# Gate products moved behind the state chains of a running head, in a two-layer decoder trunk on one core

## The chip, the cores and the metric

One core of a Trainium2 chip runs the whole program. Its engines work side by side and wait for one another by semaphores: TensorE (PE in the profile, its weight loads PEld), VectorE (DVE), ScalarE (ACT), GpSimd (POOL), and SyncE (SP), which here only issues transfers. The metric is the device time of one execution in microseconds (us), the median of several runs.

## The reference

Two layers act on 1024 tokens of width 1024, in float32. The first mixes the tokens with a gated linear recurrence of 8 heads, the second with a causal convolution module; a squared-ReLU MLP follows each, with post-normalisation. The change lies in the first mixer alone:

```python
def hgrn2_mixer(h, w_in, lb, norm_g, w_out):
    proj = h @ w_in
    q, fz, v, g = jnp.split(proj, 4, axis=-1)
    q = jax.nn.silu(q)
    f = lb + (1.0 - lb) * jax.nn.sigmoid(fz)
    log_f = jnp.log(jnp.maximum(f, GATE_EPS))
    k = 1.0 - f
    ...
    bc = jnp.cumsum(to_chunks(log_f, dk), axis=-2)
    o = chunkwise_gated_recurrence(qc, kc, vc, bc)   # S = diag(f) S + k v^T, o = S^T q
    o = o * lax.rsqrt(jnp.mean(jnp.square(o), axis=-1, keepdims=True) + RMS_EPS)
    o = o * norm_g.reshape(H, dv)
    o = o.reshape(B_, S_, D) * jax.nn.silu(g)
    return o @ w_out
```

The product in the last line but one, `o * silu(g)`, is what the change moves.

## The kernel before

**Order.** In this stage the program writes out the order of every engine by hand. TensorE runs 12 pairs of weight blocks (8 pairs of q and forget gate, `"q"`, one for each head; 4 pairs of output gates, `"g"`, each for two heads). Each pair is seven products, the forms 1, 2, 6, 5, 7, 3, 4 of a Strassen-like scheme (`ORDER`), and each product is 12 matmuls over four weight tiles. After each weight tile `slot()` runs: one tick of a counter `ticks[0]`. Work of other engines is put off by ticks with `later(n, job)`, and every call is recorded in the order in which it is made, so a job that is put off later stands later in its engine's queue.

**Forms and buffers.** `make_form` builds the weight forms: ScalarE casts a block `pr` into `fs` (L634), VectorE subtracts the cast to get the low part. `evacuate` takes the products out of PSUM. For the forms 1, 6 and 5 ScalarE copies the bank into one of four buffers `t` (L857); later forms are added to it by VectorE. Forms 1, 6, 7 and 4 accumulate in one and the same bank, so form 7 can start only when the copy of form 6 has read it. The four buffers `t` (t_755 to t_758 in the rows below) rotate: after a pair of output gates they hold the four gates `silu(g)` (two heads, two halves of the tokens), and the next pair writes them again.

**Recurrence.** Between the matmuls of the pairs, `step()` advances up to two heads at once, each by one stage of the generator `recurrence(h)`; `one[2]` in `active` counts the stages of a head. In stage 13 TensorE transposes the keys, and in stage 14 it makes the outer products of keys and values, from which VectorE forms a chain of four states (`state`: a copy and three multiply-adds). One stage later the state matmuls of TensorE use them (`ps<-state,qk`), and a second chain of three follows. Then ScalarE sums the squares of the head's outputs (L755), GpSimd raises them to the power -1/2 (L756, L538), ScalarE scales the outputs (L761), TensorE turns them (`ps<-ident,o`), ScalarE scales them again (L774), and SP writes them to memory (`od`).

**Gates.** `gate_turn()` runs on each tick. It reads an output back from `od` into one of two buffers `u`, and when the gate is there and nine ticks have passed since the read was issued, VectorE multiplies (`t<-u,t`); two ticks later SP stores the product (`zd<-t`):

```python
        if loaded and loaded[0][0] in gates and loaded[0][2] <= now - 9:
            (h, half), u, _ = loaded.pop(0)
            g = gates.pop((h, half))
            mul(g, u, g)
```

This happens 12 times, for six heads; the last two heads take another way. SP issues all transfers of this stage in one order: blocks `pr`, values `v`, outputs `od`, returned outputs `u`, products `zd`.

**Weight sums.** GpSimd's queue also carries transfers that sum blocks of the MLP's second weights in memory (`sum_w`, L419 to L423), one after another, each waiting for an earlier one to land. They stand in the same queue as GpSimd's part of the recurrence.

Of the kernel before, what the change touches and what calls it, by code (L numbers as in the profile page):

```python
# [268 lines left out]
def body(ctx, tc, d, out):  # L269
# [114 lines left out]
    def later(n, job):  # L384
        if n:
            waiting.append((ticks[0] + n, job))
        else:
            job()
# [252 lines left out]
    qk, gates, vts = {}, {}, {}  # L641

    def mul(o, a, b):
        vector.tensor_tensor(out=o, in0=a, in1=b, op=ALU.mult)
# [182 lines left out]
    recs, active, pace, alone = [], [], [0.0, 0.0], [False]  # L827
# [94 lines left out]
    def slot():  # L922
        tick()
        gate_turn()
        pace[0] += pace[1]
        if pace[0] >= 1:
            pace[0] = pace[0] - 1 if step() else 0.0

    to_load, loaded, to_gate = [], [], []

    def gate_turn():
        now = ticks[0]
        if to_load and len(loaded) < 2 and done.get(to_load[0], now) <= now - 7:
            at = to_load.pop(0)
            u = p1("u")
            nc.sync.dma_start(out=u, in_=od[at[0]][at[1]])
            loaded.append((at, u, now))
        if loaded and loaded[0][0] in gates and loaded[0][2] <= now - 9:
            (h, half), u, _ = loaded.pop(0)
            g = gates.pop((h, half))  # L940
            mul(g, u, g)

            def store():
                nc.sync.dma_start(out=zd[half][:, h, :], in_=g)
                stored[h, half] = ticks[0]

            later(2, store)
# [1035 lines left out]
```

## Time and profile before

| | |
|---|---|
| median of 3 runs | 2057.65 us (2055.35 to 2061.02) |
| profiled execution | 2057.38 us, its span 2055.6 us |
| PE busy | 2024.2 us (98%) |
| DVE busy | 1488.7 us (72%) |
| ACT busy | 1092.3 us (53%) |
| POOL busy | 394.7 us (19%) |
| the recurrence's stage, 98 to 425 us | PE busy 317.71 of 327.00 us |
| the twelve products `t<-u,t` | DVE, median 691 ns, from 198.2 to 392.9 us |

The span runs from the first to the last instruction; the time of the execution has a little on either side of it. A row of the timeline gives the start, the duration, the engine, the source line, the operation with its output and inputs, how many like it were merged, and in brackets how long the engine had stood idle before it and what ended that. Operations that go through the clock-keeping wrapper all carry the line L204, so they are told apart by their tiles. A row of waits gives the waiting instruction, what it waited for, the total in us, how often, and the longest.

### The profile page before, as it was taken

Reading aid. Unit: us, or ns where it says so; the run is one execution under the profiler, and the core shown is the slowest. Engines: PE = TensorE matmul, PEld = TensorE weight load, DVE = VectorE, ACT = ScalarE, POOL = GpSimd, SP = SyncE. Lnnn points to the kernel's source line nnn. Section 1 sums busy time; section 2 is a strip of 40 time slices with the busy share of each in tenths; the row PEclk is TensorE's granted clock in tenths of the full one; section 3 lists DMA queues with packets and bytes.
Section 4 is the critical chain, followed back from the end, with each engine's and each line's share of the span. In section 5 each row is a group of like instructions: output and inputs, shape, how many; then the busy total and the mean of one; then the engine's idle time right before and its main releaser. Section 6 shows DMA issues by size and latency. Waiting matters only on the chain. (4 is left out here: it accounts for less than half of the span.)

```text
span 2055.6 us, 29682 instructions
## 1 busy us (share of the span) xinstructions
PE 2024.2 (98%) x11144; PEld 1669.3 (81%) x11144; DVE 1488.7 (72%) x1978; ACT 1092.3 (53%) x1725; POOL 394.7 (19%) x405
## 2 busy tenths in 40 slices
PE   8999999999999999999999999999999999999998
PEld 7888887888788888888888888888888888888886
DVE  8698887877866665666557898889589666754456
ACT  5456565631654655444443776488615555443343
POOL 0112232111000000000001799079210000100002
PEclk9999999999999999999999999999999999999999
DMA  4788999942399786999998755487659778995542
GB/s 187 216 206 229 263 244 250 268 185 89 125 324 298 275 302 215 374 341 325 336 339 294 303 185 187 191 329 268 255 210 344 247 236 299 392 293 195 194 154 103
DMA packets 183120, 517.55 MB, mean 252 GB/s; under 512 B 17984, under 2 KB 49856, under 8 KB 181824
## 3 DMA queue, kind: packets, MB, share of 16 engines
q1 hardware_dynamic: 167488, 456.93, 61.7%
q0 software_dynamic: 15488, 58.72, 12.3%
q8 instruction: 87, 1.43, 0.3%
q14 instruction: 57, 0.47, 0.1%
HBM read 380.85 MB, written 201.85 MB: 283 GB/s over the span
## 5 line engine op out<-in xcount | busy, mean ns | idle before, releaser
L204 PE MATMUL ps<-dw,dh 128*128 128x512 f32 x2688 | 611.6, 389 | 0.9 <-ACT dh L72 0.7
L204 PEld LDWEIGHTS ps<-dw,dh 128*128 128x128 f32 x2688 | 504.1, 188 | 106.3 <-ACT dh L72 1.1
L204 PE MATMUL ps<-x1f,fw 128*128 128x512 f32 x1344 | 307.8, 390 | 4.3 <-ACT fw L72 2.9
L204 PEld LDWEIGHTS ps<-x1f,fw 128*128 128x128 f32 x1344 | 251.4, 188 | 59.2 <-issue 2.7
L204 PE MATMUL ps<-xf,fs 128*128 128x512 f32 x1008 | 250.0, 399 | 3.5 <-issue 1.9
L204 POOL TENSOR_TENSOR cb<-cb,prod 128x512 f32<-128x512 f32 x168 | 222.5, 1333 | 14.4 <-ACT prod L1614 4.1
L204 PEld LDWEIGHTS ps<-xf,fs 128*128 128x128 f32 x1008 | 184.8, 189 | 42.8 <-issue 2.1
L204 DVE TENSOR_TENSOR dh<-dh 128x1024 fp32r<-128x1024 f32 x112 | 136.3, 1222 | 109.6 <-ACT dh L72 106.5
L204 DVE SCALAR_TENSOR_TENSOR ps<-u,par,ps 128x512 f32<-128x512 f32 x296 | 205.9, 749 | 10.7 <-ACT ps L1626 9.3
L204 PE MATMUL ps<-xa,wa 128*128 128x512 f32 x864 | 203.6, 393 | 1.3 <-DVE xa L204 0.9
L72 ACT CAST dh<-dh 128x1024 fp32r<-128x1024 f32 x112 | 117.2, 1050 | 146.3 <-DMA dh<-hf 141.2
L204 DVE TENSOR_TENSOR dw<-dr,dw 128x1024 fp32r<-128x1024 f32 x112 | 136.2, 1222 | 76.2 <-ACT dw L72 75.5
L204 PEld LDWEIGHTS ps<-xa,wa 128*128 128x128 f32 x864 | 160.2, 188 | 35.1 <-DVE xa L204 1.3
L72 ACT CAST dw<-dr 128x1024 fp32r<-128x1024 f32 x112 | 117.1, 1052 | 134.7 <-PE ps L204 114.0
L1614 ACT ACTIVATE prod<-u,par 128x512 f32<-128x512 f32 x168 | 119.2, 725 | 35.4 <-POOL cb L204 34.8
L538 POOL TENSOR_TENSOR mv<-mv,nhalf 128x1 f32<-128x1 f32 x32 | 42.2, 1319 | 403.9 <-DVE mv L204 393.6
L204 PE MATMUL ps<-w,oT 128*128 128x512 f32 x384 | 89.9, 392 | 1.3 <-ACT oT L952 0.8
L204 PE MATMUL ps<-xb,wa 128*128 128x512 f32 x384 | 91.1, 393 | 0.0
L204 PE MATMUL ps<-vw,xf 128*128 128x512 f32 x336 | 79.4, 398 | 6.1 <-ACT vw L455 5.5
L204 PEld LDWEIGHTS ps<-w,oT 128*128 128x128 f32 x384 | 71.4, 188 | 16.6 <-ACT oT L952 1.2
L204 PEld LDWEIGHTS ps<-xb,wa 128*128 128x128 f32 x384 | 71.1, 188 | 14.4
L1465 ACT CAST spare<-next 128x1024 fp32r<-128x1024 f32 x38 | 39.9, 1051 | 78.0 <-DMA next<-in_wpw_dram 23.9
(252 smaller groups left out, 2915.3 us busy)
## 6 DMA issues: line engine op xcount, KB each, us to landing
wa<-ready SPq DMA_DIRECT2D x140, 512.0 KB, 4.4
dh<-hf SPq DMA_DIRECT2D x112, 512.0 KB, 4.7
sum_w<-in_w_dram POOLq DMA_DIRECT2D x40, 1024.0 KB, 10.8
ready<-spare SPq DMA_DIRECT2D x76, 512.0 KB, 5.0
raw<-in_w1q_dram SPq DMA_DIRECT2D x66, 512.0 KB, 4.6
dr<-sum_w SPq DMA_DIRECT2D x64, 512.0 KB, 7.4
hf<-ht SPq DMA_DIRECT2D x112, 256.0 KB, 6.1
dr<-in_w_dram SPq DMA_DIRECT2D x48, 512.0 KB, 6.9
```

The source lines that it names most:

```text
L72: self.nc.scalar.copy(out=slot[:, 0, c], in_=raw[:, c])
L204: return op(*args, **kw)
L538: nc.gpsimd.tensor_tensor(out=dst, in0=src, in1=nhalf[:, :n], op=ALU.pow)
L1465: nc.scalar.copy(out=slot[:, 0].bitcast(F32R), in_=raw)
L1614: nc.scalar.activation(tp, u[:, k : k + HT], AF.Copy, scale=tap(j, k))
```

## The change

While any running head has reached stage 13 or 14, a product is held until 18 ticks after its output's read was issued; otherwise until nine, as before.

```diff
@@ -935,7 +935,8 @@
             u = p1("u")
             nc.sync.dma_start(out=u, in_=od[at[0]][at[1]])
             loaded.append((at, u, now))
-        if loaded and loaded[0][0] in gates and loaded[0][2] <= now - 9:
+        busy = any(13 <= one[2] <= 14 for one in active)
+        if loaded and loaded[0][0] in gates and loaded[0][2] <= now - (18 if busy else 9):
             (h, half), u, _ = loaded.pop(0)
             g = gates.pop((h, half))
             mul(g, u, g)
```

On TensorE, ScalarE and GpSimd no instruction changes its place. On VectorE five of the twelve products move, in three places; on SP the stores of the products, and a few transfers beside them.

Place 1, VectorE, after the gates of heads 0 and 1 (rows of the difference; t_756 to t_758 are gate buffers, T_763 holds decay products of the younger head, fs and pr are a weight form and its block): ahead of the older head's first state stood two products.

```order
 L204 TENSOR_TENSOR fs_595<-pr_600,fs_595 128x512
-L204 TENSOR_TENSOR t_757<-u_762,t_757 128x512
 L204 SCALAR_TENSOR_TENSOR t_758<-ps_70,sq_760 128x512
-L204 TENSOR_TENSOR t_756<-u_761,t_756 128x512
 L204 COPY state_772<-ps_70 128x128
 L204 SCALAR_TENSOR_TENSOR state_773<-state_772,dec_775,ps_70 128x128
```

They now stand behind the second chain of that head, on both sides of an addition into t_755:

```order
 L204 TENSOR_TENSOR T_763<-T_763 128x64
+L204 TENSOR_TENSOR t_757<-u_762,t_757 128x512
 L204 TENSOR_TENSOR t_755<-t_755,ps_70 128x512
+L204 TENSOR_TENSOR t_756<-u_761,t_756 128x512
 L204 TENSOR_TENSOR fs_590<-pr_599,fs_590 128x512
```

Place 1, SP's queue (the line of the store differs by the line that the change adds): the store of t_756 stood among the first of these, and now stands behind the load of pr_599, which waits until VectorE has read that block's last use.

```order
 L605 DMA pr_600<-in_wp_dram 128x512
+L605 DMA pr_598<-in_wp_dram 128x512
 L936 DMA u_762<-od10_573 128x512
-L944 DMA zd1_588<-t_757 128x512
-L944 DMA zd1_588<-t_756 128x512
-L605 DMA pr_598<-in_wp_dram 128x512
+L945 DMA zd1_588<-t_757 128x512
 L605 DMA pr_599<-in_wp_dram 128x512
+L945 DMA zd1_588<-t_756 128x512
 L652 DMA v_779<-vd00_86 128x4x128
```

Both stores moved down past the load of pr_598, and that of t_756 past the load of pr_599 as well. ScalarE's next copy into t_756 is that of form 6 of the pair that runs then.

Place 2, VectorE, after the gates of heads 2 and 3: one product ahead of a first state.

```order
 L204 TENSOR_TENSOR fs_594<-pr_600,fs_594 128x512
-L204 TENSOR_TENSOR t_755<-u_762,t_755 128x512
 L204 COPY state_769<-ps_70 128x128
 L204 SCALAR_TENSOR_TENSOR state_770<-state_769,dec_776,ps_70 128x128
```

It moved behind that head's second chain. In place 3, after the gates of heads 4 and 5, one product moves from ahead of the first chain to between the first and the second.

## The prediction

> **What bounds the kernel now.** I read the page first, then two windows of the span, then what TensorE waits for inside the stage that the change touches.
>
> ```profile
> span 2055.6 us, 29682 instructions
> PE 2024.2 (98%) x11144; PEld 1669.3 (81%) x11144; DVE 1488.7 (72%) x1978; ACT 1092.3 (53%) x1725; POOL 394.7 (19%) x405
> ...
> 98.00:425.00 327.00, 317.71 (x3501) 262.56 (x3500) 272.38 (x442) 202.10 (x478) 73.80 (x86) 0.99 0.90 250
> ...
> PE ps L204 <- ACT o L761: 2.4, 3, 1.1
> PE ps L204 <- issue: 1.9, 1, 1.9
> PE ps L204 <- DVE state L204: 1.4, 2, 0.9
> ```
>
> TensorE is busy for 98% of the span, so time is won or lost only where it stands still. The row by windows is the stage of the pair products and the recurrence, 98 to 425 us: 327.00 - 317.71 = 9.3 us of TensorE idle, with the DMA engines at 0.90. That is 0.45% of the span, and no reordering here can win more. The last three rows are TensorE's longest waits from 140 to 432 us (total, times, longest). The wait that this change can remove is the third: twice, 1.4 us together, TensorE waits for the state chains. A result within 0.3% (6.2 us, about what a measurement of this kernel can tell from no change) is still "the same".
>
> **The change, place by place.** Nothing is added or removed; TensorE, ScalarE and GpSimd keep their orders. Of the 12 products of a gate with a returned output, five change position on VectorE, and their stores with them on SP's queue. There are three places.
>
> Place 1, near 218 us. Timeline rows (start, duration, and in brackets the idle time before):
>
> ```profile
> 217.08 0.68 DVE L204 TENSOR_TENSOR t<-u,t 128x512 f32<-128x512 f32 x1
> 217.68 0.68 DVE L204 SCALAR_TENSOR_TENSOR t<-ps,sq 128x512 f32<-128x512 f32 x1
> 218.28 0.68 DVE L204 TENSOR_TENSOR t<-u,t 128x512 f32<-128x512 f32 x1
> 218.88 0.28 DVE L204 COPY state<-ps 128x128 f32<-128x128 f32 x1
> ...
> 225.41 0.68 DVE L204 TENSOR_TENSOR fs<-pr,fs 128x512 fp32r<-128x512 f32 x1
> ...
> 217.68 0.60 PE L204 MATMUL ps<-v,at 128*128 128x128 f32 x4
> 219.22 0.49 PE L204 MATMUL ps<-state,qk 128*128 128x128 f32 x2 [0.94 <-DVE state L204]
> ```
>
> Two products stand right ahead of the first state; consecutive starts are 0.60 apart, so without them the copy of the state starts 1.20 us earlier, at 217.68, and ends near 217.96. TensorE is through with its four matmuls at 218.28. The 0.94 us wait goes whole. On VectorE the products return after the second chain, where the row at 225.41 again stands behind the same work and keeps its time.
>
> What is late next is what hangs on the products. The second one (buffer t_756) was done at 218.96 and is now done near 225.4. Its store stood among the first here, and in the new order it stands behind a load that waits for the row at 225.41:
>
> ```profile
> 218.16 1.15 SPq L944 DMA_DIRECT2D zd<-t  x2
> 223.34 3.12 SPq L605 DMA_DIRECT2D pr<-in_wp_dram  x2
> ...
> 228.12 0.64 ACT L857 COPY t<-ps 128x512 f32<-128x512 f32 x1
> ...
> 230.25 3.02 PE L204 MATMUL ps<-xf,fs 128*128 128x512 f32 x12
> ...
> pr<-in_wp_dram SPq DMA_DIRECT2D x2, 256.0 KB, 5.0
> ...
> u<-od SPq DMA_DIRECT2D x14, 256.0 KB, 3.6
> v<-vd SPq DMA_DIRECT2D x14, 256.0 KB, 9.9
> ...
> out_dram<-y SPq DMA_DIRECT2D x4, 256.0 KB, 2.0
> ```
>
> The second load of the pair ended at 223.34 + 3.12 = 226.46, so the store is issued at about 226.5 instead of before 219.31. ScalarE's copy at 228.12 writes the next form's sum into that same t_756 and must wait until the store has read it. Behind the copy on ScalarE stand a weight cast and the scaling of the head's outputs. The copy also empties the PSUM bank into which the product at 230.25 (form 7) accumulates. So the chain is store, copy, TensorE, and its length is the store's landing time, which the trace does not give for these stores. Four rows bound it for 256 KB: 2.0 (stores at the end of the kernel) and 9.9 (loads of the values), with 3.6 and 5.0 between. I take 5.0, because these are two transfers of the same size on the same queue in just this stretch (223 to 227 us). The store then lands at 231.5, the copy ends at 231.5 + 0.64 = 232.1, and form 7 starts 1.9 us later than before, although TensorE could have come at 230.25 - 0.94 = 229.31. At 2.0 the copy ends by 229.1 and 0.94 is kept; at 9.9 it ends at 237.0 and place 1 costs 6.8.
>
> The Trainium skill ("DMA: Bandwidth & Descriptors", section "Anatomy of one DMA") gives a fit, made on the gpsimd path, of about 2.0 us fixed plus bytes over 436 GB/s. By it 256 KB land in an estimated 2.6 us, the copy ends at 229.7 and place 1 wins 0.5 instead of losing 1.9; the loads at 5.0 in this stretch contradict it, and the final sum below comes out the same by both.
>
> VectorE's third product (t_758) moves a little too:
>
> ```profile
> 228.07 0.68 DVE L204 TENSOR_TENSOR t<-u,t 128x512 f32<-128x512 f32 x1
> ...
> 233.03 0.69 DVE L204 TENSOR_TENSOR fs<-pr,fs 128x512 fp32r<-128x512 f32 x1 [2.59 <-ACT fs L634]
> ...
> 360.86 0.59 ACT L857 COPY t<-ps 128x512 f32<-128x512 f32 x1
> ```
>
> It goes from 228.07 behind the subtraction at 233.03. ScalarE's delay reaches that subtraction as well, which then runs up to 2 us late, as TensorE does; VectorE sat idle 2.59 us ahead of it, so this adds nothing of its own. The reload of the u buffer waits for the first product and moves with it by some 6 us; what reads it is this third product, later still, so I cost it at nothing.
>
> Does the shift reach the end? The next wait of TensorE:
>
> ```profile
> 268.52 0.66 PE L204 MATMUL ps<-ident,o 128*128 128x128 f32 x4 [1.06 <-ACT o L761]
> ...
> 264.11 1.22 POOL L421 DMA_DIRECT2D sum_w<-in_w_dram  x1 [4.32 <-issue]
> 265.40 0.70 POOL L756 TENSOR_SCALAR ss<-ss 128x4 f32<-128x4 f32 x1
> 266.19 1.10 POOL L538 TENSOR_TENSOR ss<-ss,nhalf 128x4 f32<-128x4 f32 x1
> ...
> 267.32 1.14 ACT L761 ACTIVATE o<-ps,ss 128x128 f32<-128x128 f32 x4 [2.29 <-POOL ss L538]
> ```
>
> TensorE waits for ScalarE, ScalarE for GpSimd's power, and GpSimd's two operations start only when the DMA issue at 264.11 is through. That issue follows the landing of an earlier block copy: the weight sums on GpSimd's queue are a chain of transfers that does not ask where TensorE stands. So this point is a clock of its own. A lead of 0.94 is lost here (the wait becomes 2.0), and a lag of 1.9 shrinks by 1.06 to 0.8.
>
> Place 2, near 335 us, and the clock of GpSimd after it:
>
> ```profile
> 334.53 0.68 DVE L204 TENSOR_TENSOR t<-u,t 128x512 f32<-128x512 f32 x1
> 335.13 0.28 DVE L204 COPY state<-ps 128x128 f32<-128x128 f32 x1
> ...
> 335.47 0.49 PE L204 MATMUL ps<-state,qk 128*128 128x128 f32 x2 [0.51 <-DVE state L204]
> ...
> 380.62 0.86 POOL L423 DMA_DIRECT2D sum_w<-sum_w  x1 [10.90 <-DMA sum_w<-in_w_dram]
> 381.55 0.74 POOL L756 TENSOR_SCALAR ss<-ss 128x4 f32<-128x4 f32 x1
> ...
> 385.09 0.66 PE L204 MATMUL ps<-ident,o 128*128 128x128 f32 x4 [0.94 <-ACT o L761]
> ```
>
> One product ahead of the state goes behind the second chain: 0.60 earlier, more than the 0.51 that TensorE waited, so 0.5 us is won. Its store is then issued near 341.7, and its buffer is written again only by the copy at 360.86 (row above), 19 us later, so nothing waits for that one. At 385.09 the pattern of 268.52 returns: ScalarE's factor comes from GpSimd, which had waited 10.90 us for a DMA. 0.94 is absorbed.
>
> Place 3, near 372 us:
>
> ```profile
> 371.21 0.69 DVE L204 TENSOR_TENSOR t<-u,t 128x512 f32<-128x512 f32 x1
> 372.42 0.28 DVE L204 COPY state<-ps 128x128 f32<-128x128 f32 x1
> ...
> 376.94 1.11 DVE L204 SCALAR_TENSOR_TENSOR state<-state,dec,ps 128x128 f32<-128x128 f32 x3 [0.88 <-PE ps L204]
> ```
>
> Here TensorE does not wait for the state at all, and the product moves into a hole of 0.88 us ahead of the second chain. I cost it at nothing; its cover is that hole, and without it the second chain would start 0.60 later.
>
> **Sum.** Place 1 puts TensorE 1.9 later; 1.06 of it goes at 268.52, 0.8 stay; place 2 takes 0.5, 0.3 stay; at 385.09 they go into the 0.94. At the end 0.0. With a landing of 2.0 a lead arrives at both clocks and is lost there: again 0.0. The profiled execution took 2057.38, 1.8 above its span and 0.3 under the median of the three runs (2057.65), so the forecast is 2057.4.
>
> **Rivals.** Faster: the leads stay. This needs GpSimd's chain of weight sums to come earlier itself, which could be, since the stores leave 218 to 225 us, where the chain's transfers also run. Then 0.94 + 0.51 = 1.45 are won. A second source is a stall that the change might shift away:
>
> ```profile
> 347.28 1.49 PE L204 MATMUL ps<-xf,fs 128*128 128x512 f32 x4 [1.89 <-issue]
> ...
> 348.00:351.50 3.50, 3.50 (x12) 2.77 (x12) 1.92 (x5) 3.09 (x9) 1.00 (x1) 0.55 1.05 233
> ```
>
> TensorE stands 1.89 us in the middle of one product, waiting for nothing that the profile shows, and then runs 3.5 us at a granted clock of 0.55, which loses 3.5 x 0.45 = 1.6. If this goes, 3.5 us are won: 2053.9. Against it: nothing in the change touches that product. I price the rival at 2055.0, between the two gains.
>
> Slower: the late store. It decides from the landing time on. Covered are 230.25 - 0.64 - 226.5 = 3.1 us until form 7 is later than before, and 1.06 + 0.51 + 0.94 = 2.5 more by the later slack, so the end moves from a landing of 5.6 us on. At 9.9 the end is 4.3 later, 2061.7. The wait may also cost the clock: at 5.0 TensorE would idle 232.1 - 229.3 = 2.8 us, longer than the 1.89 after which the clock fell above, and 1.6 would come on top, 1.9 + 1.6 - 2.5 = 1.0 at the end, 2058.4. For the rival as a whole I take 2060. Over 0.3% slower it is only from 5.6 + 6.2 = 11.8 us of landing.
>
> On that clock the Trainium skill ("TensorE: Matmul & The Clock Gate", section "Why this matters for your kernels") says that gaps over about 3 us between bursts bring it down. By that page a stall of 2.8 us would be free and the 1.0 would not come; the row at 348 us, after 1.89 us of idle, speaks for the charge, and I leave it in the rival.
>
> No effect: the rule acts on too little. Only two of the five moved products had a wait behind them; if place 1's wait is not VectorE's order but the recurrence's own length, the time is also 2057.4. The rows at 217.08 to 218.88, back to back, speak against it.
>
> **How the numbers follow.** Likeliest, shifts absorbed: 0.58, 2057.4, own range 2055.5 to 2059.5, since the three runs differ by that much. No effect: 0.04, the same number. Faster rival: 0.17, of which 0.03 beyond 0.3%. Slower rival: 0.21, of which 0.04 beyond 0.3%. The range of 8 in 10 takes the low end of the faster rival, 2053.9, and the landing of 9.9, 2061.7. Faster 0.03, the same 0.93, slower 0.04.
>
> **What would show it.** In the new profile the two waits of the state matmuls (0.94 and 0.51) should be gone. Form 7's matmuls near 230 us should show a new wait of up to 2.8 us on ScalarE's copy into t, and that copy should start at about 231. The transposes near 268 and 385 us should again wait on ScalarE's outputs, and start within 1 us of the old times. I am wrong if the state waits remain, if the copy into t starts near 228 although the store is late, if TensorE's order near 268 or 385 no longer waits, or if the time moves by more than 6 us, which would say that a chain that I hold for paced by DMA is paced by TensorE.

## The result and the profile after

The changed kernel takes 2063.32 us (median of 22 runs, 2055.49 to 2068.91), the kernel before 2057.77 on the same chip (22 runs, 2054.29 to 2063.74). The ratio is 1.0026, 95% interval 1.0016 to 1.0035: 5.5 us slower, outside the forecast range. The profiled execution took 2062.3, with a span of 2060.5 against 2055.6. One of the twelve runs of e3 below took 2897.82 us at a granted clock of 0.65; it is left out of that kernel's ratio, and the other eleven have a median of 2060.90.

The page of the changed kernel, then TensorE's longest waits from 140 to 440 us (total, times, longest):

```profile
span 2060.5 us, 29679 instructions
PE 2024.0 (98%) x11144; PEld 1670.4 (81%) x11144; DVE 1487.8 (72%) x1978; ACT 1092.9 (53%) x1725; POOL 393.0 (19%) x405
...
PE ps L204 <- ACT t L857: 10.2, 2, 9.3
PE ps L204 <- issue: 1.3, 1, 1.3
```

TensorE's work is the same (2024.0 us). The waits for VectorE's state are gone from the list, and one wait of 9.3 us for ScalarE's copy into t has come. The timeline around it, first SP's queue and GpSimd, then ScalarE and TensorE:

```profile
224.79 0.43 SPq L945 DMA_DIRECT2D zd<-t  x1
226.22 0.33 SPq L605 DMA_DIRECT2D pr<-in_wp_dram  x1
226.60 0.47 SPq L945 DMA_DIRECT2D zd<-t  x1
...
225.67 0.92 POOL L423 DMA_DIRECT2D sum_w<-sum_w  x1 [2.58 <-DMA sum_w<-in_w_dram]
226.28 1.07 POOL L419 DMA_DIRECT2D sum_w<-in_w_dram  x1
229.49 0.76 POOL L420 DMA_DIRECT2D sum_w<-in_w_dram  x1
...
238.08 0.58 ACT L857 COPY t<-ps 128x512 f32<-128x512 f32 x1 [10.31 <-DMA zd<-t]
...
228.78 0.60 PE L204 MATMUL ps<-ident,o 128*128 128x128 f32 x4
238.72 4.94 PE L204 MATMUL ps<-xf,fs 128*128 128x512 f32 x12 [9.34 <-ACT t L857]
```

The store of t_756 is issued at 226.60, the copy that waits for it starts at 238.08: 11.5 us. The product of form 7, which took 3.02 us before, then takes 4.94. The view by windows says why (length, TensorE's busy time; the numbers near the end are granted clock, DMA share and GB/s):

```profile
228.70:232.60 3.90, 0.68 (x6) 0.36 (x3) 0.00 (x0) 0.00 (x0) 1.55 (x2) 1.00 0.90 189
232.60:243.00 10.40, 4.29 (x10) 3.40 (x11) 2.31 (x5) 3.71 (x9) 1.29 (x2) 0.51 1.05 315
```

The clock stays full for the first 3 us of the wait and is then at about half speed for some 10 us, the last 4 of them with TensorE at work. What came after the wait, by the same instruction's start in both traces:

| TensorE's instruction | before | after | later by |
|---|---|---|---|
| first state matmul, place 1 | 219.22 | 218.21 | -1.01 |
| transposes ahead of form 7 | 229.90 | 228.78 | -1.12 |
| form 7 | 230.25 | 238.72 | +8.47 |
| transposes behind it | 233.12 | 243.49 | +10.37 |
| transposes near 268 | 268.52 | 277.66 | +9.14 |
| state matmul, place 2 | 335.47 | 343.99 | +8.52 |
| transposes near 385 | 385.09 | 390.49 | +5.40 |
| first matmul of the feed-forward part (x1f) | 511.73 | 517.90 | +6.17 |
| end of the span | 2055.6 | 2060.5 | +4.9 |

The loss is made in one place, and half of it is given back. The rows that answer to the waits of before:

```profile
277.66 0.60 PE L204 MATMUL ps<-ident,o 128*128 128x128 f32 x4
343.99 0.49 PE L204 MATMUL ps<-state,qk 128*128 128x128 f32 x2
355.39 1.09 PE L204 MATMUL ps<-xf,fs 128*128 128x512 f32 x4 [1.34 <-issue]
390.49 0.60 PE L204 MATMUL ps<-ident,o 128*128 128x128 f32 x4
```

The waits of 1.06, 0.51 and 0.94 are gone: 9.14 - 10.37 = -1.2 at the first, -0.6 up to and with the second. Between 344 and 390 us 3.1 are won: the 0.94, the stall of 1.89 that is now 1.34 (0.55), and the half clock behind that stall, which had cost 1.6 and is not there now (four matmuls in 1.09 us). 0.94 + 0.55 + 1.6 = 3.1. The transposes near 268 and 385 no longer wait for ScalarE and come 9.1 and 5.4 us later, which is one of the signs of error that the prediction named.

### The profile page after: what moved, and what is told of

It reads as the page before. It is cut to its first block, busy times and chain, and to the rows that moved or that the text cites. A ratio compares the mean times of both kernels' runs of the same rounds, so it can differ in the third digit from the quotient of the medians.

```text
span 2060.5 us, 29679 instructions
## 1 busy us (share of the span) xinstructions
PE 2024.0 (98%) x11144; PEld 1670.4 (81%) x11144; DVE 1487.8 (72%) x1978; ACT 1092.9 (53%) x1725; POOL 393.0 (19%) x405
## 4 chain that ended last, share of the span: by engine, by line
PE 75%; DVE 9%; DMA 8%; issue 3%; ACT 3%; POOL 2%; SPq 0%; DVEq 0%; POOLq 0%; ACTq 0%
PE ps L204 75%; DMA raw<-in_w1q_dram 1%; POOL cb L204 1%; DMA dr<-in_w_dram 1%; DMA next<-in_w1q_dram 1%; DMA zd<-t 1%; DVE qk L204 1%; DVE t L204 1%; DMA vr<-in_wv_dram 1%; DVE y L204 1%; DVE fs L204 1%; DVE xf L204 1%; DVE fw L204 0%; DVE vr L204 0%; DMA dh<-hf 0%
## 5 line engine op out<-in xcount | busy, mean ns | idle before, releaser
L204 PEld LDWEIGHTS ps<-vw,xf 128*128 128x128 f32 x336 | 64.6, 193 | 20.7 <-ACT vw L455 5.0
```

Source lines behind the costliest of these rows:

```text
L204: return op(*args, **kw)
```

## The experiments

All times against the kernel before on the same chip. "x1f" is the start of the first matmul of the feed-forward part, behind the recurrence; "rest" is the span's end less x1f. The kernel before had medians of 2059.52 beside e1 to e4, 2057.99 beside e5 to e7, 2058.74 beside e8 and e9, and 2057.29 beside e10 and e11; the ratios are to these runs, and need not be the plain quotients of the medians.

| kernel | median us | ratio (95%) | span | x1f | rest |
|---|---|---|---|---|---|
| before | 2057.77 | | 2055.6 | 511.73 | 1543.9 |
| after | 2063.32 | 1.0026 (1.0016 to 1.0035) | 2060.5 | 517.90 | 1542.6 |
| e1 places 2, 3 | 2058.59 | 0.9993 (0.9983 to 1.0003) | 2056.9 | 513.74 | 1543.2 |
| e2 place 1 | 2068.48 | 1.0043 (1.0029 to 1.0058) | 2063.7 | 516.96 | 1546.7 |
| e3 store ahead | 2061.27 | 1.0010 (0.9997 to 1.0023) | 2062.1 | 515.71 | 1546.4 |
| e4 first chain only | 2060.38 | 1.0001 (0.9990 to 1.0013) | 2060.4 | 514.76 | 1545.6 |
| e5 block sum away | 2063.55 | 1.0028 (1.0015 to 1.0040) | 2062.1 | 511.77 | 1550.3 |
| e6 e4, addition late | 2057.79 | 0.9998 (0.9989 to 1.0008) | 2060.3 | 515.44 | 1544.9 |
| e7 before, addition late | 2056.77 | 1.0002 (0.9991 to 1.0013) | 2054.3 | 512.32 | 1542.0 |
| e8 e3, copy first | 2063.10 | 1.0021 (1.0008 to 1.0034) | 2060.8 | 512.12 | 1548.7 |
| e9 before, block sum away | 2055.74 | 0.9982 (0.9972 to 0.9993) | 2053.2 | 510.68 | 1542.5 |
| e10 e4 and e9 | 2054.86 | 0.9985 (0.9975 to 0.9996) | 2052.2 | 509.84 | 1542.4 |
| e11 e1 and e9 | 2057.19 | 1.0000 (0.9990 to 1.0009) | 2053.2 | 510.16 | 1543.0 |

Single runs of one kernel scatter over 6 to 13 us, so a median is read with its interval, and a cause from the rows of one trace.

**e1 and e2: which place.** Only heads 3 and 4, or only heads 0 and 1, hold their products back:

```diff
-        busy = any(13 <= one[2] <= 14 for one in active)
+        busy = any(13 <= one[2] <= 14 for one in active) and loaded and loaded[0][0][0] > 1   # e1; "< 2" in e2
```

> Heads 0 and 1 are treated as in the kernel before, heads 3 and 4 as in the changed one (places 2 and 3 alone). Theory A (the loss is place 1 alone: the store of t_756 issued at 226.60 lands 11.5 us later, ScalarE's copy waits for it, form 7 on TensorE waits 9.3 us for the copy and then runs at half clock): TensorE's 0.94 wait for the state near 218 is back, form 7 starts without a wait of more than 1 us, no stretch of half clock near 233 to 243, and the time is that of the kernel before, 2055 to 2059, ratio 0.999 to 1.001. Theory B (any reordering of these products costs, through VectorE's order or the reload of u that moves with them): form 7 may be whole and the time is still 2060 to 2063.

> Heads 0 and 1 are treated as in the changed kernel, heads 3 and 4 as in the one before (place 1 alone). Theory A: the whole loss is here: form 7 waits 8 to 10 us for ScalarE's copy into t, the granted clock is 0.5 for about 10 us, TensorE's 0.51 wait for the state of place 2 near 343 is back, and the time is 2061 to 2064, ratio 1.002 to 1.003. Theory B (the loss is spread over the places or sits in the later ones): 2058 to 2060, ratio about 1.001 or less.

e1 is the kernel before again (0.9993), with the 0.92 wait at place 1 back and no wait for the copy at form 7. e2 has the wait:

```profile
236.31 0.58 ACT L857 COPY t<-ps 128x512 f32<-128x512 f32 x1 [8.45 <-DMA zd<-t]
...
236.95 4.75 PE L204 MATMUL ps<-xf,fs 128*128 128x512 f32 x12 [7.48 <-ACT t L857]
...
342.64 0.49 PE L204 MATMUL ps<-state,qk 128*128 128x128 f32 x2 [0.50 <-DVE state L204]
```

So place 1 alone makes the loss (theory A), with a wait of 7.48 us a little shorter than the 8 to 10 expected. The whole time, 2068.48, is worse than theory A's 2061 to 2064. The rows say where: x1f comes 5.2 us later than before, and another 2.8 are lost behind it (rest 1546.7 against 1543.9). The order of the instructions behind the recurrence is not written by hand; it is laid by the program's scheduler from its own estimates, and in e2, e5 and e8 it came out another way: some products of the x1f stage stand in another order on TensorE, with changes on VectorE and ScalarE beside them. e8 comes back to that.

**e3: one DMA moved.** The store of t_756 is written right behind its product, so that on SP it stands ahead of the other store and of the load of pr_599:

```diff
-            later(2, store)
+            later(0 if (h, half) == (0, 1) else 2, store)
```

> The changed kernel with one DMA moved: the store of t_756 is written right behind its product, so that on SP it stands ahead of the store of t_757 and of the load of pr_599; the order on VectorE is that of the changed kernel. By the trace it can then be issued near 225.7 instead of 226.60. Theory A1 (it was late because it stood behind the load of pr_599 and shared its queue): it lands in about 5 us, near 231, form 7 waits 2 us or less, and the time is 2056 to 2059. Theory A2 (it was late because of GpSimd's block-sum transfers issued at 225.67 to 229.49, whoever is ahead of it on SP): it lands near 236 to 237, form 7 still waits 7 to 9 us, and the time is 2060 to 2063. Theory B (VectorE's order): form 7 is whole and the time is 2060 to 2063.

SP and GpSimd, ScalarE, TensorE in e3:

```profile
225.84 0.80 SPq L945 DMA_DIRECT2D zd<-t  x2
226.74 0.41 SPq L605 DMA_DIRECT2D pr<-in_wp_dram  x1
...
226.37 0.92 POOL L423 DMA_DIRECT2D sum_w<-sum_w  x1 [3.06 <-DMA sum_w<-in_w_dram]
226.98 1.07 POOL L419 DMA_DIRECT2D sum_w<-in_w_dram  x1
...
229.82 0.58 ACT L857 COPY t<-ps 128x512 f32<-128x512 f32 x1 [1.83 <-DMA zd<-t]
...
230.45 3.02 PE L204 MATMUL ps<-xf,fs 128*128 128x512 f32 x12 [0.84 <-ACT t L857]
```

The store is issued 0.76 us earlier and lands 8.3 us earlier: 4.0 us from issue to copy. The wait at form 7 falls from 9.3 to 0.84, at full clock, with VectorE's order as in the changed kernel. The wait is A1's, but the time (2061.27) lies above A1's range, and a whole form 7 at 2060 to 2063 us was the sign of theory B. The rows name two later waits: in the profiled run TensorE waits 2.09 at 269.74 for ScalarE's o and 3.11 at 398.45 for VectorE's blocks. The blocks stand behind a product on VectorE that the change does not move; it starts at 396.14, after 2.70 us of waiting for its returned output u. So these losses are waits too, but that theory B has no part in them is not shown by e3; e5 speaks to it. A1 and A2 are not told apart yet, because the store was now ahead of the load and, by half a microsecond, of GpSimd's transfers.

**e5: GpSimd's block sum moved away.** SP's order is that of the changed kernel; the one block sum whose copies were issued at 226.28 and 229.49 starts 6 ticks later, with its additions:

```diff
-        queue.dma_start(out=v[:, 0:2], in_=w[:, 0:4:2])
-        later(gap // 2, lambda: queue.dma_start(out=v[:, 2:4], in_=w[:, 0:2]))
+        later(6 if gap and (layer, c) == (0, 6) else 0, lambda: queue.dma_start(out=v[:, 0:2], in_=w[:, 0:4:2]))
+        later(gap // 2 + (6 if gap and (layer, c) == (0, 6) else 0), lambda: queue.dma_start(out=v[:, 2:4], in_=w[:, 0:2]))
...
-            later((i + 1) * gap, part)
+            later((i + 1) * gap + (6 if gap and (layer, c) == (0, 6) else 0), part)
```

> The changed kernel with the one block sum whose first copies GpSimd issued at 226.28 and 229.49 put off by 6 ticks (some 12 us), with its additions; the store of t_756 stays where it is on SP, behind the load of pr_599. In the stretch 226 to 238 GpSimd then has only 512 KB additions under way and not 2 MB of copies. Theory A2 (GpSimd's transfers take the DMA engines from the store): it lands in 4 to 6 us, form 7 waits 2 us or less, at full clock, and TensorE's first x1f matmul, which stood at 511.73 before and 517.90 after, comes at 512 to 515. Theory A1 (its place behind the load of pr_599): it lands after 9 to 12 us, form 7 waits 7 to 9 us and x1f comes at 516 to 518. The later order of TensorE and VectorE (beyond 511 us) differs a little from the changed kernel's, so the whole time says less than these rows: 2056 to 2060 by A2, 2061 to 2066 by A1.

```profile
226.37 0.33 SPq L605 DMA_DIRECT2D pr<-in_wp_dram  x1
226.75 0.49 SPq L945 DMA_DIRECT2D zd<-t  x1
...
227.06 0.92 POOL L423 DMA_DIRECT2D sum_w<-sum_w  x1 [3.82 <-DMA sum_w<-in_w_dram]
229.65 0.78 POOL L419 DMA_DIRECT2D sum_w<-in_w_dram  x1
...
231.47 0.58 ACT L857 COPY t<-ps 128x512 f32<-128x512 f32 x1 [3.55 <-DMA zd<-t]
...
232.11 4.35 PE L204 MATMUL ps<-xf,fs 128*128 128x512 f32 x12 [2.58 <-ACT t L857]
```

Behind the same load, issued even 0.15 us later than in the changed kernel, the store now lands after 4.7 us. That is A2: what is ahead of it on the DMA engines decides, not its place behind the load. Form 7 waits 2.58 and then runs slowly (4.35 us), a little more than the 2 us at full clock that A2 said. x1f comes at 511.77, 6.1 earlier than in the changed kernel and level with before, although VectorE keeps the changed kernel's order all through the recurrence; that leaves little for theory B. About 1 us of it may be the edit's own, since it brings x1f forward by 1.05 in the kernel before as well (e9). The whole time, 2063.55, misses A2's 2056 to 2060, and it is lost behind x1f: the rest takes 1550.3, in the other order, where TensorE now waits for ScalarE in the x1f stage. From 505 us on, first before, where that wait was 0.2 (once), then e5 (the same line of the program, one further down by the line that the change adds):

```profile
PE ps L204 <- ACT c L1286: 0.2, 1, 0.2
```

```profile
PE ps L204 <- ACT c L1287: 4.9, 4, 1.6
```

**e8: the copy ahead of the store, the store ahead of the load.** e3, with the additions of the block sum before put off by 2 ticks, which lets the next sum's copy go out first:

```diff
-            later((i + 1) * gap, part)
+            later((i + 1) * gap + (2 if gap and (layer, c) == (0, 5) else 0), part)
```

> The kernel that stores t_756 ahead of the load of pr_599 (e3), and on GpSimd the additions of the block sum before put off by 2 ticks, so that the next one's first copy of 1 MB is issued ahead of them, some 4 us earlier than in e3 (near 223 instead of 226.98), before the store of t_756. Nothing else in the recurrence moves; beyond 511 us TensorE, VectorE and SP stand in the order of e2 and e5, not in that of the kernel before. Theory A2 (GpSimd's copies take the DMA engines): the store, ahead of the load as in e3, now lands after 7 us or more instead of 4.0, and form 7 waits 3 us or more. Theory A1 (the place on SP's queue decides): it lands in 4 to 5 us as in e3, form 7 waits 1 us. Theory L (the later order costs by itself): from TensorE's first x1f matmul to the end of the span 1547 to 1550 us pass, as in e2 and e5 (1546.7 and 1550.3), where the kernels with the order of before took 1542.0 to 1546.4; if not, 1542 to 1546, and what e5 lost there was chance.

```profile
223.01 0.78 POOL L419 DMA_DIRECT2D sum_w<-in_w_dram  x1
...
225.57 1.46 SPq L945 DMA_DIRECT2D zd<-t  x2
...
233.10 0.59 ACT L857 COPY t<-ps 128x512 f32<-128x512 f32 x1 [5.36 <-DMA zd<-t]
...
233.74 4.38 PE L204 MATMUL ps<-xf,fs 128*128 128x512 f32 x12 [4.39 <-ACT t L857]
```

The same store in the same place on SP as in e3 now needs 7.5 us instead of 4.0, because 1 MB of GpSimd's was issued 2.6 us ahead of it: A2, on a second arrangement. And the rest takes 1548.7 us, in the order of e5: theory L's number. The three kernels with the other order took 1546.7, 1550.3 and 1548.7 behind x1f, the others 1542.0 to 1546.4, and their wait for c was 3.6 to 4.9 us against at most 1.9. The two groups nearly touch and each kernel has one trace, so that the later order costs by itself is likely, but not shown.

Put together, the landing of the 256 KB store of t_756 (issue to the start of the copy that waited for it) against what of GpSimd was under way at its issue:

| kernel | store issued | GpSimd's transfers ahead of it | copy starts | landing |
|---|---|---|---|---|
| after | 226.60 | additions 512 KB at 225.67, copy 1 MB at 226.28 | 238.08 | 11.5 |
| e2 | 226.69 | the same, at 226.00 and 226.61 | 236.31 | 9.6 |
| e6 | 223.37 | additions 1 MB from 216.82, landed 229.40 | 231.04 | 7.7 |
| e11 | 219.42 | additions 1 MB from 216.18 | 230.52 | 11.1 |
| e7 | 218.44 | additions 1 MB from 216.38, landed by 228.21 | 227.99 | 9.6 |
| e8 | 225.57 | copy 1 MB at 223.01 | 233.10 | 7.5 |
| e5 | 226.75 | none (the next at 227.06) | 231.47 | 4.7 |
| e3 | 225.84 | none (the next at 226.37) | 229.82 | 4.0 |

In e7 and e11 the products of heads 0 and 1 stand where they stood in the kernel before, and there too the copy had to wait for the store:

```profile
227.99 0.59 ACT L857 COPY t<-ps 128x512 f32<-128x512 f32 x1 [0.26 <-DMA zd<-t]
...
230.52 0.58 ACT L857 COPY t<-ps 128x512 f32<-128x512 f32 x1 [1.82 <-DMA zd<-t]
```

So a landing of some 10 us occurs in the old place too, where the copy comes some 9 us after the issue and hides nearly all of it. In e4 and e10 additions of 1 MB (from 215.14 and 216.05) were under way as well when the store was issued (223.11, 223.70), but they had landed by 225.09 and 225.90, about 2 us later; the copy did not wait, so the store took at most 4.4 and 4.6 us. The landing thus goes with how much of GpSimd's traffic is still to come, and not with whether any is ahead.

The split of the DMA engines' time while the store was under way shows the same: the changed kernel from 226.6 to 238.1, and e3 from 225.8 to 229.9 (packets, MB, share of the 16 engines; q0 is GpSimd's queue, q1 that of SP):

```profile
q0 software_dynamic: 562, 2.18, 68.6%
q1 hardware_dynamic: 732, 0.94, 25.2%
```

```profile
q1 hardware_dynamic: 549, 0.99, 78.4%
q0 software_dynamic: 19, 0.08, 25.9%
```

**e4: the products behind the first chain only.** This keeps the gain at place 1 and brings the stores 3.5 us forward:

```diff
-        busy = any(13 <= one[2] <= 14 for one in active)
+        busy = any(one[2] == 13 for one in active)
```

> The products are held back for the first of the two chains only: they stand behind the first chain of the older head's state and ahead of its next cast pair and its second chain, so that the stores of t_757 and t_756 can be issued near 220 to 223, some 4 us earlier than in the changed kernel and ahead of GpSimd's transfers of 225.67. Theory A (store to copy to form 7): it lands by 231 at the latest, form 7 waits less than 1 us, no half clock near 233 to 243; of the 0.94 wait at place 1 part stays gone; the time is 2055 to 2058, ratio 0.998 to 1.000. If the store lands late all the same (11 us from 222 is 233) form 7 waits 4 us and the time is 2059 to 2061. Theory B (any reordering costs): 2060 to 2063.

The copy into t starts at 227.52 without a wait, TensorE waits neither for a state at place 1 nor for the copy at form 7. The time is that of the kernel before (2060.38 against 2059.52, 1.0001); it lies above theory A's 2055 to 2058 and within theory B's 2060 to 2063, though the rows are theory A's. The lead was lost at the next place, GpSimd, ScalarE and TensorE near 268:

```profile
266.34 1.22 POOL L421 DMA_DIRECT2D sum_w<-in_w_dram  x1 [6.85 <-issue]
267.64 0.19 POOL L756 TENSOR_SCALAR ss<-ss 128x4 f32<-128x4 f32 x1
...
268.98 1.14 ACT L761 ACTIVATE o<-ps,ss 128x128 f32<-128x128 f32 x4 [5.36 <-POOL ss L538]
...
270.17 1.12 PE L204 MATMUL ps<-ident,o 128*128 128x128 f32 x4 [4.13 <-ACT o L761]
```

GpSimd's two small operations for ss stand behind the issue of an addition that itself could not go out for 6.85 us. This is the clock of its own of the prediction, and it is later here than before (TensorE starts at 270.17 against 268.52).

**e6 and e7: that issue behind ss.** The first addition of each block sum goes out 3 ticks later, in e4 and in the kernel before; TensorE, VectorE and SP keep their orders:

```diff
-            later((i + 1) * gap, part)
+            later((i + 1) * gap + (3 if i == 0 and gap else 0), part)
```

> The kernel that holds the products back for the first chain only, and on GpSimd the first addition of each block sum put off by 3 ticks, so that the two small operations for ss near 267 stand ahead of it in GpSimd's queue; every other engine's order stays. Theory G (the lead that TensorE wins early is lost near 268 because GpSimd's ss stands behind a DMA issue that itself waits, 6.85 us in that run): the 4.13 wait for ScalarE's o at 270.17 falls below 1 us, no half clock there, x1f comes 3 to 4 us earlier than its 514.76, and the time is 2055 to 2057 with the before of 2059 to 2060, ratio 0.997 to 0.999. Theory H (ss is late through ScalarE or TensorE itself, or the lead is lost again at the next place near 385): the wait at 270 goes but comes back later, ratio 0.9995 to 1.001.

> The kernel before with the same move on GpSimd alone: the first addition of each block sum 3 ticks later, ss ahead of it. Theory G: TensorE's 1.06 wait at 268.52 goes and nothing gives it back but the 0.94 at 385.09: 0 to 1.5 us faster, ratio 0.9993 to 1.000; the products held back then add what e6 gains beyond this (their 0.94 and 0.51 waits, and the stall near 347). Theory H: no change at all, 1.000, with the wait still at 268.

The wait near 268 is gone in both (e7 has none there, e6 at most 0.4 for ScalarE's o anywhere from 140 to 440 us), so GpSimd's order did make it. But neither becomes measurably faster: 0.9998 and 1.0002, theory H's number by theory G's mechanism. In e6's trace the lead goes to the store's landing once more (7.7 us, form 7 waits 2.4) and to a 2.08 wait for the loads of the values at 406.29, behind which eight matmuls take 2.05 us instead of the 1.13 of e7; in e7's, the 0.94 at 384.32 is there as before.

**e9, e10 and e11: the block sum away, where nothing waits for the store.** e9 is the kernel before with e5's edit; e10 and e11 are e4 and e1 with it. All three keep the order of before behind x1f on TensorE.

> The kernel before with the block sum's copies put off by 6 ticks, as in e5 (no product is held back, and the order beyond 511 us is that of the kernel before). Theory A2: moving the copies costs nothing by itself, since no store is waited for here near 226 to 238: 2055 to 2060, ratio 0.999 to 1.001. If the block sum's own lateness costs something (GpSimd's later transfers, ss behind them), ratio over 1.001 and a new wait for ScalarE's o between 240 and 300.

> e4 and e9 together: the products held back for the first chain only, and the block sum's copies put off by 6 ticks. Every order beyond 511 us is that of the kernel before. Theory A2 with G (leads last once neither the store's landing nor GpSimd's ss stands in the way): e9's profile had 0.93 and 0.47 of TensorE's waits for the state left, and nothing between 240 and 330; with these gone the first x1f comes 1 to 1.5 us ahead of e9's 510.68, and the ratio to the kernel before is 0.997 to 0.998 where e9 had 0.9982. Rival (something else takes the lead back before 511 us, such as the store's landing at 7 us or the loads of the last heads' values near 405): the ratio is e9's or worse, 0.998 to 1.000, with the new wait in the rows.

> e1 and e9 together: heads 3 and 4 with their products held back, heads 0 and 1 as before, and the block sum's copies put off by 6 ticks. By the rows the 0.47 wait for the state near 335 goes and the 0.93 near 220 stays: x1f 0.5 us ahead of e9's 510.68, ratio 0.9975 to 0.9985, the same as e9 within what can be measured. Rival: as for the other kernel, 0.998 to 1.000.

e9 was expected to change nothing and is faster than before, 0.9982 (0.9972 to 0.9993): with the sum later GpSimd is free when ss comes, and the waits of 1.06 and 0.94 near 268 and 385 are both gone. e10 beats both kernels: 2054.86 us, 0.9985 (0.9975 to 0.9996) of before. Its longest waits from 140 to 440 us:

```profile
PE ps L204 <- issue: 2.1, 1, 2.1
PE ps L204 <- ACT kt L744: 0.9, 2, 0.5
PE ps L204 <- ACT t L857: 0.9, 1, 0.9
```

Its x1f at 509.84 is 1.9 us ahead of before and 0.8 ahead of e9, less than the 1 to 1.5 expected, and its ratio cannot be told from e9's: what holding the products back adds there was not shown by the times. e11 missed: its profiled run has the early x1f (510.16), yet its runs give 1.0000. In that run the copy into t waited 1.82 us for the landing of the store issued at 219.42, so the store can be late there too; whether that is what happens in its other runs stays open.

## Why the prediction was wrong

- **The state waits** (0.94 at place 1, 0.51 at place 2): gone, as said; TensorE was 1.0 ahead at 218 and 1.1 at 229. Place 3 cost nothing.
- **The late store**: issued at 226.60 (forecast 226.5), and the chain store, ScalarE's copy, bank, form 7 is the one that bound. That mechanism was right.
- **Its landing, taken as 5.0, is the step that failed.** It was 11.5, outside the bounds of 2.0 to 9.9 as well, so form 7 came 8.5 later and not 1.9. The 5.0 was that of loads on the same queue; but no row of before said what a store takes when GpSimd's transfers are issued just ahead of it, and the copy at 228.12 bounded the old landing only from above, at some 9 us, because it had not waited. e5 and e8 show that these transfers make the difference: 4.7 without them behind the same load, 7.5 with them ahead of the same load. By the fit in the Trainium skill ("DMA: Bandwidth & Descriptors", section "Anatomy of one DMA"), made on the gpsimd path, 256 KB take an estimated 2.6 us. The nearest landing measured here is e3's 4.0, and no run here shows a store with the DMA engines to itself. GpSimd's transfers were to be seen in the trace of before, a little ahead of the 226.5 that was forecast for the store, but the landing was priced from SP's rows alone:

```profile
225.79 0.92 POOL L423 DMA_DIRECT2D sum_w<-sum_w  x1 [1.59 <-DMA sum_w<-in_w_dram]
226.40 1.07 POOL L419 DMA_DIRECT2D sum_w<-in_w_dram  x1
```

- **The clock** was named, priced at 1.6, and left in the slower rival. It cost 1.9: form 7 took 4.94 against 3.02. That rival gave 4.3 at 9.9 us; with 11.5 its own rule (11.5 - 5.6) gives 5.9, near the 4.9 of the trace and the 5.5 of the medians, but by luck: the clock's cost and the 2.15 of the next point nearly cancel.
- **The absorbers** (1.06, 0.51, 0.94) all gave about what was said, and the stall near 347 gave 2.15 more, which the faster rival had priced and set aside because nothing touches it. It differs between kernels that do not touch it either: 1.34 and no half clock in the changed kernel, 0.35 in e1, 2.19 and no half clock in e4. What sets it stays open.
- **GpSimd's clock of its own** was half right. It does not ask where TensorE stands, e4 shows, but it is no fixed time either: in the changed kernel ss at 267.95 waited for ScalarE, and in e6 and e9 another place in GpSimd's queue takes the wait away.

## What to carry to other kernels

A transfer that is moved later meets other traffic: before pricing its landing, look at what every queue issues in the new place, GpSimd's bulk copies first, and take a row's duration only from a transfer with the same company. A buffer that was written again without a wait says only that its store had landed by then; the slack that hid a slow store goes with the move. And where the order of two DMAs makes the loss, moving one of them by a microsecond can be worth more, at that place, than the wait that the change was made for: 0.76 us in e3 brought form 7 forward by 8.3, and the wait was 0.94.

## What the runs showed of the hardware that was not expected

- A 256 KB store to memory landed in 4.0 and 4.7 us with nothing of GpSimd's queue ahead of it (e3, e5), and in 7.5 to 11.5 us behind 1 to 1.5 MB of its copies and additions (e6, e7, e8, e11, e2, after); while the changed kernel's store waited, the queue of GpSimd held 68.6% of the DMA engines' time and SP's queue 25.2%. Between the changed kernel and e3, an issue 0.8 us earlier went with a landing 7.5 us shorter.
- TensorE's granted clock fell to about half after idle times of 1.89 (before), 2.09 (e3), 2.12 (e10), 2.37 (e6), 2.58 (e5), 4.13 (e4) and 9.34 us (after), and not after 0.84 (e3) or 1.34 (after). Length alone does not decide, though: behind the same stall near 347 us the clock stayed full after 1.87 (e5), 1.97 (e7), 2.15 (e6) and 2.19 us (e4), and near 405 us after 2.35 (e1). So the 1.6 us of half clock that went away near 347 in the changed kernel need not be the shorter stall's doing. The Trainium skill ("TensorE: Matmul & The Clock Gate", section "Why this matters for your kernels") puts the gap at over about 3 us; here 1.89 us was enough once, and 2.35 was not enough another time.
